# Low parts of two MLP products by an adding DMA, in a decoder block on one Trainium2 core

## The chip, the core and the metric

The kernel runs on one core of a Trainium2 chip. The core has a matrix engine (TensorE, PE in the profile), a vector engine (VectorE, DVE), a scalar engine (ScalarE, ACT), GpSimd (POOL) and SyncE (SP), which issues transfers. Each engine works through its own instructions in the order in which they stand, and waits on semaphores for the others. Sixteen DMA engines move data between HBM and the on-chip memory SBUF; products accumulate in PSUM banks.

The metric is the device time of one execution in microseconds (us). Before the change it is 862.61 us, the median of three runs (862.43 to 863.16).

## The reference

One decoder block over 512 tokens of width 1024, all in float32: two branches (stick-breaking attention, RWKV-7), a squared-ReLU MLP, a gated embedding and a final norm. The change lies in the MLP, whose second product is `... @ w_ff2`:

```python
D_MODEL = 1024; SEQ = 512; D_FF = 4 * D_MODEL
h = rms_norm(x, mlp_norm_g[i])
x = x + jnp.square(jax.nn.relu(h @ w_ff1[i])) @ w_ff2[i]     # the MLP
gate = jax.nn.sigmoid(rms_norm(x, ple_norm_g[i]) @ w_ple_gate[i])
x = x + gate * (p[i] @ w_ple_proj[i])
return rms_norm(x, final_norm_g)
```

## The kernel before

**Split operands.** TensorE multiplies in a short float format (`float32r`). To keep float32 accuracy each operand is two tiles, a high part (the value cast to `float32r`) and a low part (the value minus the high part, cast too), and each product is three matmuls: high by high, high by low, low by high.

**Weights.** They are cut into units of 128 x 1024 floats (512 KB). The list `seq` holds the order in which units are used. For a unit, `fetch_to` has SP load it from HBM into `w_raw` (four buffers), has ACT cast it into `w_hi` (line 221, three buffers), and has DVE subtract to make `w_lo` (line 222, three buffers). A cast therefore has to wait until PE is done with the unit three places earlier. `step` calls `fetch_to` after the third step of the unit in use, so that the next units are asked for ahead.

**The MLP.** The hidden width is worked through in four quarters (`qd` 0 to 3). In a quarter the first product makes 1024 hidden columns: pairs of units (`FF1`), some of them by a scheme with seven block products in place of eight (`seven`); the last pair of each quarter is always two whole units of 24 matmuls of 512 columns. Relu and square (`squared`, ACT) and sums and splits of the results (`operands`) follow.

The second product of a quarter (`FF2`) is seven block products (`seventh`, i = 0 to 6), each with two units (`p_` = 0 and 1): fourteen units in a row, each used by twelve matmuls of 512 columns (`rows3`, lines 252 to 254: high by high, low weights, low rows). Products 0 and 1 use units as they are loaded. Products 2 and 4 use sums of units that were prepared earlier in `B11a`, `B11b`, `B12a`, `B12b`. Products 3 and 6 subtract such a sum from the loaded unit first, and 5 uses its units as loaded. A unit is written (i, p_) here; those of products 0 and 1 are (0,0), (0,1), (1,0) and (1,1). In the trace their rows operands are named `fA` (products 0, 1 and 6) and `fS` (products 2 to 5).

**What sets the order.** The program is recorded in the order of the Python code, and a scheduler then places each engine's instructions by when it reckons them ready. So a change of one operation can move others on every engine. Nothing of the order is read for time here: times come from the trace.

The other work on ACT beside the casts, where products 0 and 1 begin: relu and square of the last `FF1` unit, the high parts of the rows (`fA`, `fS`), and in quarter 0 the high parts `tb` of sums of the normed input, which later quarters use.

Of the kernel before, what the change touches and what calls it, by code (L numbers as in the profile page):

```python
# [13 lines left out]
AF = mybir.ActivationFunctionType  # L14
ALU = mybir.AluOpType
# [25 lines left out]
U_PLE, U_QKV, U_RW, U_GSB, U_GRW, U_UPSB, U_UPRW, U_OUT, U_FF1, U_FF2, U_GATE = range(11)  # L41
# [50 lines left out]
def tile_block(ctx: ExitStack, tc: tile.TileContext, xT, xt, pT, wts, lora, cols_d, gfin_d, consts_d, out, dbg=None):  # L92
    nc = tc.nc
    act, dve, pool, pe, sync = nc.scalar, nc.vector, nc.gpsimd, nc.tensor, nc.sync
# [3 lines left out]
    def r32(ap):  # L98
        return ap.bitcast(F32)
# [34 lines left out]
    seq = []  # L134
# [31 lines left out]
    def unit(i):  # L166
        if seq[i][0] == U_FF2:
            return wts[UBASE[U_FF2] + seq[i][1] * 8 + FF2_FROM[seq[i][2]] + seq[i][3]]
        if seq[i][0] == U_S12:
            return wts[UBASE[U_FF1] + seq[i][1] * 8 + seq[i][2] + 4]  # L170
        return wts[UBASE[seq[i][0]] + seq[i][1]]

    def load_to(n):
        while len(loaded) < min(n, len(seq)):
            i = len(loaded)
            loaded.append(None)
            if seq[i] not in sources and seq[i][0] not in (U_S3, U_S4):
                loaded[i] = wpool.tile([P, 1024], F32, name="w_raw", bufs=4)
                sync.dma_start(out=loaded[i], in_=unit(i))
# [11 lines left out]
    def made(i):  # L191
        kind = seq[i][0]
        if seq[i] in sources:
            return sources[seq[i]]()
        if kind == U_S12:
            four_sums(i)
            return sums12[seq[i][1:]][:, 0:2].rearrange("p s x -> p (s x)")
        if kind == U_S3:
            return loaded[i - 1]
        if kind == U_S4:  # L200
            return sums12.pop(seq[i][1:])[:, 2]
        if seq[i] in changed:
            changed[seq[i]](loaded[i])
        return loaded[i]

    def fetch_to(n, ahead=0):
        while state["i"] < min(n, len(seq)):
            i = state["i"]
            state["i"] += 1
            load_to(i + 1 + ahead)  # L210
            raw = made(i)
            if seq[i] in homes:
                hi, lo = homes[seq[i]]()
            elif seq[i][0] == U_S4:
                hi = wpool.tile([P, 512], F32R, name="w_hi4", bufs=1)
                lo = wpool.tile([P, 512], F32R, name="w_lo4", bufs=1)
            else:
                hi = wpool.tile([P, 1024], F32R, name="w_hi")
                lo = wpool.tile([P, 1024], F32R, name="w_lo")
            with tc.issue_after(state["hx"]) if seq[i] == (U_FF1, 4) else nullcontext():  # L220
                state["cast"] = act.copy(out=hi, in_=raw).ins  # L221
            dve.tensor_tensor(out=lo, in0=raw, in1=r32(hi), op=ALU.subtract)  # L222
            ready.setdefault(seq[i], []).append((hi, lo))

    def weights(*u):
        assert seq[state["used"]] == u, (seq[state["used"]], u)
        state["used"] += 1
        fetch_to(state["used"])
        state["due"] = 3
        return ready[u].pop(0)  # L230
# [11 lines left out]
    def step():  # L242
        state["due"] -= 1
        if state["due"] == 0:
            fetch_to(state["used"] + AHEAD - 1, 1)
# [77 lines left out]
    with ExitStack() as sA:  # L323
# [43 lines left out]
        with ExitStack() as s1:  # L367
# [47 lines left out]
            for i in range(2):  # L415
                ready[seq[i]] = [tuple(first_w[i])]
            fetch_to(3)

            for k in range(KT):
# [1171 lines left out]
```

## Time and profile before

| What | Value |
|---|---|
| Time, median of three runs | 862.61 us (862.43 to 863.16) |
| Profiled execution: from its first to its last instruction (span) | 861.2 us |
| Granted TensorE clock, mean | 0.997 |
| PE busy / DVE busy / ACT busy / POOL busy | 845.6 / 716.8 / 497.2 / 74.4 us |
| DMA, mean rate | 131 GB/s |
| First `FF2` matmul of the four quarters, from the span's start | 522.7, 603.4, 682.8, 762.2 us |
| Transfers issued by POOL | none |

The profile has no time of the profiled execution other than its span; the median of the runs is 1.4 us longer than that span. "Busy" is the time in which an engine has an instruction under way. Matmuls overlap, so that one lasts 0.39 us but the next begins 0.23 us after it. In a timeline row the columns are the start and the length in us, the engine, the line, the operation, the tiles (out<-in), and in brackets the idle time before it with what ended it. Waits are what an engine idled for, in all, how often, and the longest. For a transfer, "to landing" is the time from its issue to the semaphore that says its data is there. Lines carry the numbers of the kernel before; in the kernel after the change those behind line 222 are four higher.

### The profile page before, as it was taken

What the parts mean: (1) busy time and instruction counts of PE and PEld (TensorE: products, weight loads), DVE (VectorE), ACT (ScalarE), POOL (GpSimd) and SP (SyncE); (2) the same over time, 40 slices, a digit from 0 to 9 for tenths busy, and PEclk for the clock granted to TensorE, in tenths of its full rate; (3) what the DMA queues carried; (4) which work ended last, traced back from release to release, by engine and by line L of the source; (5) the groups of instructions that cost most, each with busy time, mean ns of one, the idle gap of its engine ahead of it and who ended that gap; (6) DMA issues with size and microseconds to landing.
All of it is one profiled execution on the core that took longest, in us unless ns stands there. A gap on an engine that the chain in (4) does not pass through costs nothing.

```text
span 861.2 us, 14225 instructions
## 1 busy us (share of the span) xinstructions
PE 845.6 (98%) x5462; PEld 694.2 (81%) x5462; DVE 716.8 (83%) x1271; ACT 497.2 (58%) x777; POOL 74.4 (9%) x138
## 2 busy tenths in 40 slices
PE   8999999999999999999999999999999999999996
PEld 5778788877777777877888888889889889988885
DVE  7989987896987988867763599999889989998767
ACT  7878887744436253534555665457547744773843
POOL 1332431001202111020000000000000000000000
PEclk9999999999999999999999999999999999999998
DMA  8312212231221314428950643654364555444502
GB/s 319 100 49 62 87 62 85 74 99 51 62 88 37 111 63 138 159 86 277 324 186 20 245 123 100 217 172 143 118 205 133 161 188 166 140 144 128 192 23 98
DMA packets 37027, 112.67 MB, mean 131 GB/s; under 512 B 4192, under 2 KB 4192, under 8 KB 36960
## 3 DMA queue, kind: packets, MB, share of 16 engines
q1 hardware_dynamic: 36960, 111.76, 39.1%
q8 instruction: 43, 0.70, 0.3%
q14 instruction: 24, 0.20, 0.1%
HBM read 101.26 MB, written 10.49 MB: 130 GB/s over the span
## 4 chain that ended last, share of the span: by engine, by line
PE 83%; DVE 12%; issue 2%; ACT 1%; DMA 1%; SPq 0%; POOL 0%; POOLq 0%; DVEq 0%; ACTq 0%
PE ps_m L237 14%; PE ps_m L238 14%; PE ps_m L239 14%; PE ps_m L253 8%; PE ps_m L254 8%; PE ps_m L252 8%; DVE w_lo L222 2%; PE ps_g L863 1%; PE ps_o L543 1%; PE ps_s L991 1%; PE ps_z L551 1%; PE ps_c L982 1%; PE ps_g L953 1%; DVE LX L885 1%; DVE own L874 1%
## 5 line engine op out<-in xcount | busy, mean ns | idle before, releaser
L221 ACT CAST w_hi<-w_raw 128x1024 fp32r<-128x1024 f32 x131 | 137.4, 1051 | 160.1 <-PE ps_m L238 92.0
L222 DVE TENSOR_TENSOR w_lo<-w_raw,w_hi 128x1024 fp32r<-128x1024 f32 x131 | 159.8, 1223 | 26.6 <-ACT w_hi L221 26.0
L237 PE MATMUL ps_m<-h_hi,w_hi 128*128 128x512 f32 x320 | 130.5, 409 | 1.1 <-ACT h_hi L399 0.6
L239 PE MATMUL ps_m<-h_hi,w_lo 128*128 128x512 f32 x320 | 128.4, 401 | 0.0
L238 PE MATMUL ps_m<-h_lo,w_hi 128*128 128x512 f32 x320 | 128.0, 400 | 0.0
L238 PE MATMUL ps_m<-hx,w_hi 128*128 128x512 f32 (+1 forms) x224 | 77.1, 344 | 0.1
L237 PE MATMUL ps_m<-hx,w_hi 128*128 128x512 f32 (+1 forms) x224 | 77.1, 344 | 0.0
L239 PE MATMUL ps_m<-hx,w_lo 128*128 128x512 f32 (+1 forms) x224 | 77.0, 344 | 0.0
L237 PEld LDWEIGHTS ps_m<-h_hi,w_hi 128*128 128x128 f32 x320 | 60.7, 190 | 12.6 <-ACT h_hi L399 1.3
L239 PEld LDWEIGHTS ps_m<-h_hi,w_lo 128*128 128x128 f32 x320 | 60.2, 188 | 11.9
L238 PEld LDWEIGHTS ps_m<-h_lo,w_hi 128*128 128x128 f32 x320 | 60.4, 189 | 10.7 <-DVE h_lo L400 0.9
L253 PE MATMUL ps_m<-w_lo,fS 128*128 128x512 f32 x128 | 49.8, 389 | 0.0
L254 PE MATMUL ps_m<-w_hi,fS 128*128 128x512 f32 x128 | 49.8, 389 | 0.0
L252 PE MATMUL ps_m<-w_hi,fS 128*128 128x512 f32 x128 | 49.6, 389 | 0.0
L238 PEld LDWEIGHTS ps_m<-hx,w_hi 128*128 128x128 f32 x224 | 42.5, 190 | 5.3 <-DVE hx L1098 0.4
L237 PEld LDWEIGHTS ps_m<-hx,w_hi 128*128 128x128 f32 x224 | 42.5, 190 | 5.1 <-ACT hx L1097 0.2
L239 PEld LDWEIGHTS ps_m<-hx,w_lo 128*128 128x128 f32 x224 | 42.4, 190 | 5.0
L1456 POOL TENSOR_SCALAR r<-s 128x1 f32<-128x1 f32 x1 | 0.5, 517 | 475.3 <-DVE t L1436 475.3
L253 PE MATMUL ps_m<-w_lo,fA 128*128 128x512 f32 x96 | 37.7, 392 | 0.3 <-DVE w_lo L222 0.3
L254 PE MATMUL ps_m<-w_hi,fA 128*128 128x512 f32 x96 | 37.5, 391 | 0.0
L252 PE MATMUL ps_m<-w_hi,fA 128*128 128x512 f32 x96 | 37.4, 391 | 0.0
L1359 DVE TENSOR_TENSOR xs<-ps_m,xs 128x512 f32<-128x512 f32 x56 | 36.3, 682 | 0.2 <-PE ps_m L254 0.2
(405 smaller groups left out, 2083.9 us busy)
## 6 DMA issues: line engine op xcount, KB each, us to landing
w_raw<-in_wts_dram SPq DMA_DIRECT2D x146, 512.0 KB, 3.5
gates<-gg SPq DMA_DIRECT2D x16, 256.0 KB, 2.0
x_in<-in_xT_dram SPq DMA_DIRECT2D x8, 256.0 KB, 5.7
tmp<-gates SPq DMA_DIRECT2D x8, 256.0 KB, 3.2
upsb<-tmp SPq DMA_DIRECT2D x8, 256.0 KB, 4.6
ga<-upsb SPq DMA_DIRECT2D x8, 256.0 KB, 5.0
gb<-gates SPq DMA_DIRECT2D x8, 256.0 KB, 5.0
xs<-in_xt_dram SPq DMA_DIRECT2D x4, 512.0 KB, 5.3
```

What stands on the lines that cost most here:

```text
L221: state["cast"] = act.copy(out=hi, in_=raw).ins
L222: dve.tensor_tensor(out=lo, in0=raw, in1=r32(hi), op=ALU.subtract)
L237: pe.matmul(ps, wh, xh[:, k, t], start=first, stop=False, skip_group_check=skip)
L238: pe.matmul(ps, wh, xl[:, k, t], start=False, stop=False, skip_group_check=skip)
L239: pe.matmul(ps, wl, xh[:, k, t], start=False, stop=last, skip_group_check=skip)
L252: pe.matmul(ps, xh[:, k + j], wh, start=first and j == 0, stop=False, skip_group_check=True)
L253: pe.matmul(ps, xh[:, k + j], wl, start=False, stop=False, skip_group_check=True)
L254: pe.matmul(ps, xl[:, k + j], wh, start=False, stop=last and j == 1, skip_group_check=True)
L543: pe.matmul(ps_o[:, j * P:T], vv[:, j, hh, :, :].rearrange("p a d -> p (a d)"), part[:, ZB[j]:ZB[j] + ZN[j]], start=j == 2 and part is wh, ...
L551: pe.matmul(zt[b][:, :n], tri, part[:, s:s + n], start=False, stop=False, skip_group_check=True)
L863: last = pe.matmul(ps[rows, k], left[rows, k, :], rhs[rows, k], start=True, stop=True)
L1359: state["anchor"] = dve.tensor_tensor(out=xb, in0=pss[t2], in1=xb, op=ALU.add).ins
```

## The change

For the units of products 0 and 1 of the second MLP product, in all four quarters, `w_lo` is no longer made by DVE. ACT writes minus `w_hi` into `w_lo`, and then a DMA that POOL issues reads the raw unit from HBM a second time and adds it to what stands in `w_lo`. All other units are made as before. That is 4 units in each of 4 quarters: 16 DVE subtractions are gone, 16 ACT instructions and 16 transfers of 512 KB, issued by POOL, are added.

```diff
             with tc.issue_after(state["hx"]) if seq[i] == (U_FF1, 4) else nullcontext():
                 state["cast"] = act.copy(out=hi, in_=raw).ins
-            dve.tensor_tensor(out=lo, in0=raw, in1=r32(hi), op=ALU.subtract)
+            if seq[i][0] == U_FF2 and seq[i][2] in (0, 1):
+                act.activation(out=lo, in_=r32(hi), func=AF.Copy, scale=-1.0)
+                pool.dma_start(out=lo, in_=unit(i), accum_op=ALU.add)
+            else:
+                dve.tensor_tensor(out=lo, in0=raw, in1=r32(hi), op=ALU.subtract)
             ready.setdefault(seq[i], []).append((hi, lo))
```

The change also moves instructions. Three places show it.

On ACT, in quarter 0, where the second product begins. Before, from the cast of unit (1,0), `w_hi_5499`, on (`r_5439` is relu and square of the last `FF1` unit):

```order
L221 CAST w_hi_5499<-w_raw_5454 128x1024
L1250 ACTIVATE r_5439<-ps_m_5444 128x512
L1251 ACTIVATE r_5439<-r_5439 128x512
L1263 CAST tb0_5124<-tsum_5223 128x1024
L267 CAST fA20_5126<-r_5439 128x512
L221 CAST w_hi_5515<-w_raw_5497 128x1024
L221 CAST w_hi_5535<-B11a_5228 128x1024
L267 CAST fS0_5128<-sums_5477 128x1024
L221 CAST w_hi_5553<-B11b_5400 128x1024
```

And now, with the cast of (1,0) as the first row, `w_hi_5501`; (1,1) is `w_hi_5518`:

```order
L221 CAST w_hi_5501<-w_raw_5455 128x1024
L1267 CAST tb0_5124<-tsum_5223 128x1024
L1254 ACTIVATE r_5440<-ps_m_5445 128x512
L223 ACTIVATE w_lo_5502<-w_hi_5501 128x1024
L1255 ACTIVATE r_5440<-r_5440 128x512
L221 CAST w_hi_5518<-w_raw_5499 128x1024
L271 CAST fA20_5126<-r_5440 128x512
L223 ACTIVATE w_lo_5519<-w_hi_5518 128x1024
L271 CAST fS0_5128<-sums_5479 128x1024
L221 CAST w_hi_5539<-B11a_5228 128x1024
```

Line 223 is the new copy of minus high. The cast of `tb`, which stood behind relu and square, now stands ahead of them and of the copy for (1,0).

On ACT in quarter 2, from the cast of (1,0), `w_hi_6987`, on (quarters 1 and 3 read alike there, to the second copy):

```order
L221 CAST w_hi_6987<-w_raw_6941 128x1024
L1254 ACTIVATE r_6926<-ps_m_6931 128x512
L223 ACTIVATE w_lo_6988<-w_hi_6987 128x1024
L1255 ACTIVATE r_6926<-r_6926 128x512
L221 CAST w_hi_7004<-w_raw_6985 128x1024
L271 CAST fA20_5126<-r_6926 128x512
L271 CAST fS0_5128<-sums_6965 128x1024
L223 ACTIVATE w_lo_7005<-w_hi_7004 128x1024
```

No `tb` stands there; the copy for (1,0) comes behind relu, the one for (1,1) behind two casts of row operands.

On PE in quarter 0, unit (1,0), `w_hi_5499`, before:

```order
L252 MATMUL ps_m_5524<-w_hi_5499,fA20_5126 128x512
L253 MATMUL ps_m_5524<-w_lo_5500,fA20_5126 128x512
L254 MATMUL ps_m_5524<-w_hi_5499,fA21_5127 128x512
L252 MATMUL ps_m_5524<-w_hi_5499,fA20_5126 128x512
L253 MATMUL ps_m_5524<-w_lo_5500,fA20_5126 128x512
```

And as now placed:

```order
L256 MATMUL ps_m_5528<-w_hi_5501,fA20_5126 128x512
L256 MATMUL ps_m_5529<-w_hi_5501,fA20_5126 128x512
L257 MATMUL ps_m_5528<-w_lo_5502,fA20_5126 128x512
L258 MATMUL ps_m_5528<-w_hi_5501,fA21_5127 128x512
L256 MATMUL ps_m_5528<-w_hi_5501,fA20_5126 128x512
```

The row with `w_lo_5502` is the third of the unit; before, the low part was read by the second. Of unit (1,1) PE does the two first rows, then two rows (quarter 0) or six (the other quarters) of product 2, and only then the first row with its low part. On POOL, at the end of its queue, the transfers stand one behind another:

```order
L1002 TENSOR_SCALAR Sg<-S_1573,gc__3396 64x64 x2
L1002 TENSOR_SCALAR Sg<-S_1574,gc__3396 64x64 x2
L224 DMA w_lo<-in_wts_dram 128x1024 x16
L1460 TENSOR_SCALAR r_8157<-s_8156 128x1
L1461 TENSOR_SCALAR r_8157<-s_8156 128x1
```

Nothing else of POOL is queued between its last work of the RWKV branch and the end of the kernel.

## The prediction

> **What bounds the kernel now.** I read the busy times first, then the chain that ended last, then the stretches of the MLP, and last the waits of PE.
>
> ```profile
> PE 845.6 (98%) x5462; PEld 694.2 (81%) x5462; DVE 716.8 (83%) x1271; ACT 497.2 (58%) x777; POOL 74.4 (9%) x138
> ...
> PE 83%; DVE 12%; issue 2%; ACT 1%; DMA 1%; SPq 0%; POOL 0%; POOLq 0%; DVEq 0%; ACTq 0%
> ```
>
> PE is busy for 845.6 of 861.2 us. The chain gives DVE 12%, which might tempt one to relieve it. The stretches say where that matters (columns: stretch, its length, then busy time and count of PE, PE's loads, DVE, ACT, POOL, then the granted clock, DMA share and rate). The four are the second products of the four quarters:
>
> ```profile
> 522.70:559.00 36.30, 36.01 (x158) 29.36 (x157) 35.80 (x41) 18.12 (x20) 0.00 (x0) 1.00 0.47 153
> 603.40:640.00 36.60, 36.60 (x162) 30.16 (x162) 30.42 (x36) 17.32 (x18) 0.00 (x0) 1.00 0.51 169
> 682.80:719.00 36.20, 36.20 (x160) 29.84 (x159) 30.44 (x38) 16.83 (x18) 0.00 (x0) 1.00 0.54 170
> 762.20:799.00 36.80, 36.80 (x163) 30.35 (x162) 30.24 (x35) 18.30 (x19) 0.00 (x0) 1.00 0.40 122
> ...
> PE ps_m L253 <- DVE w_lo L222: 0.3, 1, 0.3
> ```
>
> DVE is nearly full in quarter 0 (35.80 of 36.30) and has about 6 us free in each of the others, yet PE has no hole except 0.3 us, once, for a low part of line 222. PE itself bounds the MLP, at full clock. So taking work from DVE can give back 0.3 us at most, and any low part that arrives late is paid in full, since PE runs in order and has no reserve.
>
> **The change part by part.** *Removed*: 16 DVE subtractions.
>
> ```profile
> L222 DVE TENSOR_TENSOR w_lo<-w_raw,w_hi 128x1024 fp32r<-128x1024 f32 x131 | 159.8, 1223 | 26.6 <-ACT w_hi L221 26.0
> ...
> L1319 ACT ACTIVATE r<-r 128x1024 f32<-128x1024 f32 x8 | 8.5, 1061 | 4.5 <-DVE r L1318 4.5
> ```
>
> 16 x 1.22 = 19.5 us of DVE, all beside PE: worth the 0.3 us above, no more. *Added on ACT*: 16 copies; the ACTIVATE of the same 128x1024 takes 1.06 us, so 17 us, of which ACT has the room (18 of 36 us busy). Without that room they would push casts back; what they do push is counted below. *Added on POOL and the DMA engines*: 16 transfers. POOL has nothing else queued there, and SP's queue is not passed.
>
> What decides is when the low part is there against when PE asks for it. A unit's cast has to wait for PE to release the buffer three units back. Unit (0,0) is cast two whole `FF1` units ahead of its use, 10.9 us, and (0,1) 8.2 us; (1,0) and (1,1) have only two `FF2` units ahead of them. ACT where quarters 0 and 2 start:
>
> ```profile
> 522.64 1.06 ACT L221 CAST w_hi<-w_raw 128x1024 fp32r<-128x1024 f32 x1 [1.84 <-PE ps_m L238]
> 523.60 0.59 ACT L1250 ACTIVATE r<-ps_m 128x512 f32<-128x512 f32 x1
> 524.22 0.63 ACT L1251 ACTIVATE r<-r 128x512 f32<-128x512 f32 x1
> 524.76 1.06 ACT L1263 CAST tb<-tsum 128x1024 fp32r<-128x1024 f32 x1
> ...
> 682.79 1.05 ACT L221 CAST w_hi<-w_raw 128x1024 fp32r<-128x1024 f32 x1 [1.61 <-PE ps_m L238]
> 683.75 0.59 ACT L1250 ACTIVATE r<-ps_m 128x512 f32<-128x512 f32 x1
> 684.37 0.63 ACT L1251 ACTIVATE r<-r 128x512 f32<-128x512 f32 x1
> ```
>
> and PE where unit (1,0) begins, in quarter 0 and in quarter 2, with the sum that `tb` waits for:
>
> ```profile
> 523.51 1.22 DVE L1221 TENSOR_TENSOR tsum<-tsum,hx 128x1024 f32<-128x1024 f32 x1
> ...
> 528.27 0.39 PE L252 MATMUL ps_m<-w_hi,fA 128*128 128x512 f32 x1
> 528.49 0.39 PE L253 MATMUL ps_m<-w_lo,fA 128*128 128x512 f32 x1
> ...
> 688.42 0.39 PE L252 MATMUL ps_m<-w_hi,fA 128*128 128x512 f32 x1
> 688.65 0.39 PE L253 MATMUL ps_m<-w_lo,fA 128*128 128x512 f32 x1
> ```
>
> Call L the time from the end of the copy of minus high to the moment when PE sees the sum landed.
>
> Quarters 1 to 3 (read in quarter 2; the first `FF2` matmul is at 682.83): in the new order cast, relu, copy. The copy takes the place of the square, 684.37, and ends at 685.43. PE now puts two high matmuls first, so that the first low one is due at 688.42 + 2 x 0.23 = 688.88. The stall is L - 3.45.
>
> Quarter 0: in the new order the `tb` cast stands ahead of relu and of the copy. It waits for `tsum`, which ended at 524.73; one subtraction (1.2 us) ahead of it on DVE goes away and a short sum waits for the later square, so I take 523.7 for it, and the `tb` cast ends at 524.75, relu at 525.4, the copy at 526.5. The low part is due at 528.27 + 0.46 = 528.73. The stall is L - 2.2.
>
> Unit (1,1): its cast waits for the square behind the copy. In quarter 2 that gives square 686.0, cast 687.0, two row casts 688.55, copy 689.6. PE, once (1,0) has landed at 685.43 + L, does ten more matmuls of it, two of (1,1) and six of product 2, 18 x 0.23 = 4.1 us, and asks at 689.5 + L; the sum lands at 689.6 + L. In quarter 0: copy until 529.85 against 526.5 + 14 x 0.23 = 529.7. About 0.1 us each. That is, the second sum travels while the first is awaited and computed, and costs next to nothing more. What stands behind the copies on ACT, the casts for product 2, ends by 690 to 692 and is asked for at about 688.2 + L: covered, as long as L is over 4, by the stall itself.
>
> Together: 4 L - 2.2 - 3 x 3.45 + 0.4 - 0.3 = 4 L - 12.5 us, where no L makes a quarter negative.
>
> L is what this trace does not have: there is no transfer issued by POOL in it, and none that adds. The nearest rows are SP's plain loads of the same 512 KB (issue; minimum, median, maximum to landing), the same size issued in pairs, the rate at which the DMA engines run when full, and POOL's shortest instruction:
>
> ```profile
> L179 SPq DMA_DIRECT2D w_raw<-in_wts_dram x76: 327/328/504, 486.4 to 817.0; - x76
> ...
> DMA to landing us min/median/max: 3.3/3.5/7.1
> ...
> DMA to landing us min/median/max: 3.7/4.9/5.2
> ...
> 12.00:16.00 4.00, 3.98 (x18) 2.98 (x17) 4.00 (x8) 4.00 (x8) 0.00 (x0) 1.00 1.04 417
> ...
> 854.65 0.52 POOL L1456 TENSOR_SCALAR r<-s 128x1 f32<-128x1 f32 x1 [475.27 <-DVE t L1436]
> ```
>
> From below L is 3.3, the quickest plain load: an adding transfer reads the same bytes from HBM and more. From above I take two loads in turn, one for each operand, the second at the slowest landing seen: 3.5 + 7.1 = 10.6, as if nothing overlapped. Between them: 3.5 for a plain load, 1.26 for a second operand of 524 KB at 417 GB/s (it has to be read out of `w_lo`), 0.5 for POOL where SP needs 0.33 (POOL's shortest row), and 0.7, half of the 1.4 us by which paired loads land later, since loads for the next units fall in the same stretch (DMA share 0.40 to 0.54). That is 6.0 us, an estimate.
>
> The page "DMA: Bandwidth & Descriptors" of the Trainium skill (section "Anatomy of one DMA — SWDGE (gpsimd) path") speaks against the change too, but more mildly: for a transfer issued by GpSimd it gives 2.0 us plus the bytes at 436 GB/s, which for twice 512 KB would be an estimate of L = 4.4 and 4 x 4.4 - 12.5 = 5 us lost. No run here shows such a transfer yet.
>
> With L = 6.0 the stalls are 3.8 us in quarter 0 and 2.6 us in each other quarter, and the sum 4 x 6.0 - 12.5 = 11.5 us. The profiled span of 861.2 becomes 872.7, and the median of the runs, which stands 1.4 us above that span, 862.6 + 11.5 = **874.1 us**.
>
> **The rivals.**
>
> *A. The add lands like a plain load* (L 3.3 to 4.9). For it: DMA engines stand half idle in these stretches (shares 0.40 to 0.54). Against it: it has an operand more to read, and POOL to pass. Time: quarter 0 loses 1.1 to 2.7, the others nothing to 1.45 each, so 863.7 to 869.7.
>
> *B. The add is much slower than two reads, or the stall costs the clock* (L 7.5 to 10.6, or a stall that throttles). For it: the clock falls soon after PE stops.
>
> ```profile
> 1.31 5.29 PE L382 MATMUL ps_z<-warm 128*128 128x512 bf16 x12 [1.31 <-POOL warm L379]
> ...
> 853.40:856.60 3.20, 0.12 (x2) 0.00 (x0) 2.84 (x11) 2.57 (x5) 0.99 (x2) 0.96 0.22 82
> 856.60:861.20 4.60, 0.00 (x0) 0.00 (x0) 0.94 (x2) 0.72 (x1) 0.00 (x0) 0.50 0.46 171
> ```
>
> PE's last matmul ended at 853.5 and the granted clock was 0.50 some 3 us later. Coming back costs about what the start shows: 12 matmuls in 5.29 us, 0.44 each against 0.23 later, 2.6 us lost. At L = 6.0 only quarter 0 stands idle for longer than 3 us; from L = 6.5 on all do, and then 4 x 2.6 = 10.4 us come on top: 886.5 at L = 6.5. Without the clock, L = 7.5 to 10.6 gives 880 to 892. Against it: the slowest load of 512 KB in the MLP took 7.1.
>
> The page "TensorE: Matmul & The Clock Gate" (section "Part 1: The HAM clock gate (the "warmup" mystery)") of the Trainium skill has the rule for this rival: after an idle window of about 3.4 us the clock is halved, and as long a busy one restores it. The end of this trace agrees, with the fall after some 3 us; by the page's window one fall would cost 1.7 us in place of 2.6, and four would give 883.
>
> *C. Not slower: the sums land in time.* One mechanism: the copy of minus high is done by 685.4 in quarters 1 to 3 and PE asks at 688.9, so that a transfer with L under 2.2 in quarter 0 and under 3.45 in the others costs nothing, and PE keeps at most its 0.3 us: 862.3. With L up to 3.4 the loss stays at 1.2 us, within what can be told. For it: 3.3 was seen. Against it: that was the quickest of 84 plain loads. Faster than 0.3 us it cannot get, because PE had no more holes; only a different order elsewhere could do that.
>
> **How the numbers follow.** The forecast (L 4.9 to 7.5 without the clock, 869.7 to 880) has a chance of 0.5, A 0.2, B 0.17, C 0.13. Differences under 0.2%, 1.7 us, can't be told from none. Faster by more has 0.03 (C's remainder), within has 0.10 of C and 0.02 of A, 0.12, and slower the rest, 0.85. The range reaches from 864.5 (A at L = 3.6) to 889 (B at L = 9.7): it leaves out most of C and the far end of B. The predicted time is that of the forecast.
>
> **What would show it.** Right: PE idle in front of the matmul with `w_lo` and `fA` of the second pair of units, eight waits or fewer, the longest in quarter 0, about 3.8 us and three of 2.6, put down to a transfer; transfers of POOL that land 5 to 7 us after the copy; DVE about 20 us less busy and ACT 17 more; everything outside `FF2` as before. Wrong: PE as gapless as before (C); waits in front of (0,0) or (0,1), which have 8 us and more, if the transfers wait for one another or POOL is slow at issuing them; a granted clock under 1 inside the MLP (B); or waits of PE on ACT or DVE at product 2, which would mean that the copies push casts back further than I reckoned.

## The result, and the profile after

The kernel after the change takes 884.02 us (median of four runs, 882.24 to 888.73), beside 862.88 us for the kernel before on the same chip. The ratio is 1.0254, with a 95% interval of 1.0230 to 1.0278: slower, by 21.1 us. Forecast were 874.1 us, 11.5 us more than before, and a range of 864.5 to 889. One execution of the kernel with product 0 alone (below) took 1676 us, with every matmul twice as long, for a reason that nothing here shows; the times below leave it out, and the 8.5 us in one expectation, which take it in, are 7.6 without it.

The profiled execution is the longest of the four, 888.73 us with a span of 887.0 us, 25.8 us over the span before. Its busy times, the chain that ended last, and the row of the adding transfers among the queues (packets, MB, their time as a share of 16 engines' span):

```profile
PE 854.2 (96%) x5462; PEld 698.2 (79%) x5462; DVE 701.7 (79%) x1255; ACT 510.6 (58%) x793; POOL 88.6 (10%) x154
...
q0 software_dynamic: 2304, 8.39, 5.6%
...
PE 75%; issue 9%; DVE 8%; DMA 5%; ACT 1%; SPq 0%; POOLq 0%; POOL 0%; DVEq 0%; ACTq 0%
```

DVE is 15 us less busy, ACT 13 more (forecast were 20 and 17), and neither shows in the time. PE is busy for 8.6 us longer with the same 5462 matmuls, and 17.0 us of idle time are new, in front of one line (PE's waits: us in all, how often, the longest):

```profile
PE ps_m L257 <- DMA w_lo<-in_wts_dram: 17.0, 8, 4.8
```

17.0 and 8.6 are the 25.8 us, nearly. The eight waits in PE's timeline (line 257 takes the low weights; in brackets the idle time before):

```profile
533.60 0.50 PE L257 MATMUL ps_m<-w_lo,fA 128*128 128x512 f32 x1 [3.04 <-DMA w_lo<-in_wts_dram]
614.29 0.50 PE L257 MATMUL ps_m<-w_lo,fA 128*128 128x512 f32 x1 [1.60 <-DMA w_lo<-in_wts_dram]
618.34 0.50 PE L257 MATMUL ps_m<-w_lo,fA 128*128 128x512 f32 x1 [0.78 <-DMA w_lo<-in_wts_dram]
692.99 0.50 PE L257 MATMUL ps_m<-w_lo,fA 128*128 128x512 f32 x1 [0.52 <-DMA w_lo<-in_wts_dram]
696.95 0.50 PE L257 MATMUL ps_m<-w_lo,fA 128*128 128x512 f32 x1 [0.92 <-DMA w_lo<-in_wts_dram]
705.07 0.80 PE L257 MATMUL ps_m<-w_lo,fA 128*128 128x512 f32 x1 [4.84 <-DMA w_lo<-in_wts_dram]
787.37 0.55 PE L257 MATMUL ps_m<-w_lo,fA 128*128 128x512 f32 x1 [3.71 <-DMA w_lo<-in_wts_dram]
793.79 0.50 PE L257 MATMUL ps_m<-w_lo,fA 128*128 128x512 f32 x1 [1.58 <-DMA w_lo<-in_wts_dram]
```

Four of them, at 533.60, 618.34, 705.07 and 793.79, are at unit (1,0), as forecast, 10.2 us together. The other four are at (0,0) and (0,1), which I had called covered. The copies and the transfers themselves (an instruction's nanoseconds: minimum, median, maximum; then us from issue to landing):

```profile
L223 ACT ACTIVATE w_lo<-w_hi 128x1024 fp32r<-128x1024 f32 x16 | 16.8, 1053 | 0.1
...
L224 POOL DMA_DIRECT2D w_lo<-in_wts_dram x16: 865/865/1031, 516.3 to 787.3; - x16
...
DMA to landing us min/median/max: 5.5/7.3/10.3
```

The copies cost what was reckoned, 1.05 us each. POOL starts a transfer 0.3 us after the copy's end, so the median L is 7.6 us where I took 6.0. Transfer by transfer, L was 5.8, 6.3, 9.6 and 10.8 us at (1,0) in quarters 0 to 3, a mean of 8.1, and 5.8 to 9.4 at the others.

PE's longer busy time is mostly a slower clock. The stretches of PE after three of the waits (length, PE busy and matmuls, granted clock, DMA share, rate):

```profile
535.10:538.50 3.40, 3.40 (x9) 0.50 0.62 122
538.50:541.90 3.40, 3.40 (x16) 1.00 0.00 0
702.30:709.10 6.80, 4.03 (x10) 0.50 0.45 84
787.70:791.10 3.40, 3.40 (x9) 0.50 1.02 257
```

In 3.4 us PE does 9 matmuls at half clock and 16 at the full one. One more such stretch, at 306 us, lies ahead of the MLP, where the change adds nothing; the second product of quarter 0 began 1.7 us later than before (524.36 against 522.70). In these stretches PE did 3.4 + 3.4 + 4.0 + 3.4 us of work, and half of it, 7.1 us, is what the clock cost. The rest of the 8.6 us goes with the waits: the matmul ahead of a wait runs out alone, 0.39 less 0.23 us each time.

### The profile page after: what moved, and what is told of

Read it like the earlier page. It is cut to its first block, busy times and chain, and to the rows that moved or that the text cites. A ratio compares the mean times of both kernels' runs of the same rounds, so it can differ in the third digit from the quotient of the medians.

```text
span 887.0 us, 14281 instructions
## 1 busy us (share of the span) xinstructions
PE 854.2 (96%) x5462; PEld 698.2 (79%) x5462; DVE 701.7 (79%) x1255; ACT 510.6 (58%) x793; POOL 88.6 (10%) x154
## 3 DMA queue, kind: packets, MB, share of 16 engines
q0 software_dynamic: 2304, 8.39, 5.6%
## 4 chain that ended last, share of the span: by engine, by line
PE 75%; issue 9%; DVE 8%; DMA 5%; ACT 1%; SPq 0%; POOLq 0%; POOL 0%; DVEq 0%; ACTq 0%
PE ps_m L241 12%; PE ps_m L242 12%; PE ps_m L243 12%; PE ps_m L257 8%; PE ps_m L258 8%; PE ps_m L256 7%; DMA w_lo<-in_wts_dram 4%; PE ps_g L867 1%; PE ps_o L547 1%; PE ps_s L995 1%; PE ps_c L986 1%; DVE w_lo L226 1%; PE ps_z L555 1%; PE ps_g L957 1%; DVE LX L889 1%
## 5 line engine op out<-in xcount | busy, mean ns | idle before, releaser
L226 DVE TENSOR_TENSOR w_lo<-w_raw,w_hi 128x1024 fp32r<-128x1024 f32 x115 | 140.5, 1224 | 19.8 <-ACT w_hi L221 18.8
L257 PE MATMUL ps_m<-w_lo,fA 128*128 128x512 f32 x96 | 40.4, 421 | 17.0 <-DMA w_lo<-in_wts_dram 17.0
L224 POOL DMA_DIRECT2D w_lo<-in_wts_dram x16 | 14.0, 878 | 393.1 <-ACT w_lo L223 167.7
L258 PE MATMUL ps_m<-w_hi,fA 128*128 128x512 f32 x96 | 39.5, 412 | 0.0
L257 PEld LDWEIGHTS ps_m<-w_lo,fA 128*128 128x128 f32 x96 | 19.3, 201 | 24.9 <-DMA w_lo<-in_wts_dram 20.8
```

The costliest lines, as they stand in the source:

```text
L224: pool.dma_start(out=lo, in_=unit(i), accum_op=ALU.add)
L257: pe.matmul(ps, xh[:, k + j], wl, start=False, stop=False, skip_group_check=True)
L258: pe.matmul(ps, xl[:, k + j], wh, start=False, stop=last and j == 1, skip_group_check=True)
```

## The experiments

Three questions stood open: is the add slow or the way over POOL (the copy and the half-size runs); is it only the landing against the lead, or do traffic, copies and POOL cost something by themselves (one product alone, the first product's units, the later low matmuls, fewer loads beside); and what the clock adds (the fillers). Each expectation says what its two theories are.

### The same transfers without the addition

```diff
-                pool.dma_start(out=lo, in_=unit(i), accum_op=ALU.add)
+                pool.dma_start(out=lo, in_=unit(i))
```

> All sixteen transfers stay with POOL, at the same size and place, but they write the raw unit over the copy of minus high in place of adding to it. Left out is the addition, so the low part holds the raw weights here; nothing else differs. Theory 1 (the add is slow: its second operand has to be read and written back by the DMA engines): landings come down to those of SP's plain loads plus POOL's 0.5 us more of issue, 4.0 to 5.5 us after the copy; stalls of 1 to 3 us a quarter, 4 L - 12.5 = 3.5 to 9.5 us, no fall of the clock: 866 to 872 us. Theory 2 (what is slow is the way over POOL, whether it adds or not): landings of 5.5 to 10.3 us as before, and 880 to 886 us.

Measured: 869.63 us (868.19 to 870.62), before 863.29, ratio 1.0069 (1.0041 to 1.0096). Its page and the answer on the transfers:

```profile
q0 software_dynamic: 2304, 8.39, 3.2%
...
L224 POOL DMA_DIRECT2D w_lo<-in_wts_dram x16: 527/527/757, 513.6 to 772.1; - x16
...
DMA to landing us min/median/max: 3.7/4.5/7.1
...
PE ps_m L257 <- DMA w_lo<-in_wts_dram: 5.1, 4, 1.7
...
770.21 0.50 PE L257 MATMUL ps_m<-w_lo,fA 128*128 128x512 f32 x1 [1.67 <-DMA w_lo<-in_wts_dram]
```

Theory 1 as it stood there, that the add is slow, holds. With as many bytes in as many packets, the packets take 3.2% in place of 5.6% of the engines' time: 16 x 866.4 x 0.032 / 2304 = 0.19 us each against 16 x 887.0 x 0.056 / 2304 = 0.34. POOL's instruction falls from 865 to 527 ns, the median landing from 7.3 to 4.5 us. Three of the four waits that stay are at (1,0), in quarters 0 to 2; the longest, shown above, is at (0,1) in quarter 3, where L was 7.4, and (1,0) of that quarter waited for nothing. The clock is whole. L at (1,0) was 4.0, 4.5, 5.1 and 5.4 us, a mean of 4.7, and the prediction's 4 L - 12.5 gives 6.5 us for it; the runs lost 6.3 by their median, and the profiled one 5.2.

The Trainium skill, page "DMA: Bandwidth & Descriptors", section "Anatomy of one DMA — SWDGE (gpsimd) path", has 2.0 us plus bytes at 436 GB/s for a transfer of POOL, 3.2 us for this one, an estimate; the fastest of these plain ones took 3.7 and the median 4.5, and the adding ones 5.5 and 7.3.

### Half the columns by the add, half by DVE

```diff
-                act.activation(out=lo, in_=r32(hi), func=AF.Copy, scale=-1.0)
-                pool.dma_start(out=lo, in_=unit(i), accum_op=ALU.add)
+                act.activation(out=lo[:, 0:512], in_=r32(hi[:, 0:512]), func=AF.Copy, scale=-1.0)
+                pool.dma_start(out=lo[:, 0:512], in_=unit(i)[:, 0:512], accum_op=ALU.add)
+                dve.tensor_tensor(out=lo[:, 512:1024], in0=raw[:, 512:1024], in1=r32(hi[:, 512:1024]), op=ALU.subtract)
```

> For the same sixteen units only the first 512 columns of the low part come by the copy and the adding transfer (256 KB, rows of 2 KB), the other 512 by DVE's subtraction. Theory 1 (the time in the air grows with the bytes, as a packet that adds takes 0.35 us for 4 KB where one that only writes takes 0.19): half the packet time, 8 x 0.17 = 1.4 us less, and a copy half as long, 0.5 us less: landings of 4 to 6 us, waits of about 1 us a quarter: 865 to 871 us. Theory 2 (the way over POOL costs the same for any size: its instruction, the first packet 1.6 us later, the number of packets): landings stay above 5 us and only the 0.5 us of the copy is won per wait, 877 to 882 us.

Measured: 875.7 us (874.72 to 880.88), before 863.23, ratio 1.0158 (1.0126 to 1.0190): between the two theories.

```profile
q0 software_dynamic: 2304, 4.20, 3.1%
...
DMA to landing us min/median/max: 3.9/5.2/6.4
...
PE ps_m L258 <- DMA w_lo<-in_wts_dram: 9.6, 8, 2.2
```

Half the bytes land 2.1 us sooner by the median, and a packet takes 0.19 us, as long as a plain one of twice the size. But over 5 us stay for a quarter of a megabyte. The landings, 3.9 to 6.4 us, are close to theory 1's 4 to 6, but the waits are not: 9.6 us in place of some 4, and neither theory's time was right. On a straight line through the two sizes, an estimate, the part that grows with the bytes is 2.1 of the 5.2 us here and 4.2 of the 7.3 at full size; some 3 us stay, which no run here splits up (POOL, the first packet, the wait for other transfers).

### One product at a time

Product 1 alone (`== 0` in place of `== 1` for product 0 alone):

```diff
-            if seq[i][0] == U_FF2 and seq[i][2] in (0, 1):
+            if seq[i][0] == U_FF2 and seq[i][2] == 1:
```

> Only units (1,0) and (1,1) get their low parts by the adding transfer; those of product 0 are DVE's again. Theory 1 (own landing time against own lead): (1,0) is asked for 2.2 us after the copy in quarter 0 and 3.45 us in the others, its sums keep landing 5.8 to 10.8 us after the copy, and the stalls sum to about 11 us as in the trace after the change, or more in quarters 1 and 3, where waits at product 0 had given (1,0) more time: 4 x 8.1 - 12.5 = 20 us, 875 to 885 us. Theory 2 (pile-up): (1,0) is now the first adding transfer of its quarter and lands after 5.5 to 6.5 us in all four: 4 x 6 - 12.5 = 11.5 us, 872 to 877 us, and only quarter 0 stands long enough for the clock to fall.

Measured: 879.48 us (877.05 to 881.11), ratio 1.0177 (1.0147 to 1.0206), 16 us more than before. The landings and the waits in PE's timeline:

```profile
DMA to landing us min/median/max: 5.5/6.3/8.5
```

```profile
530.31 0.50 PE L257 MATMUL ps_m<-w_lo,fA 128*128 128x512 f32 x1 [2.46 <-DMA w_lo<-in_wts_dram]
614.45 0.51 PE L257 MATMUL ps_m<-w_lo,fA 128*128 128x512 f32 x1 [2.04 <-DMA w_lo<-in_wts_dram]
619.93 0.50 PE L257 MATMUL ps_m<-w_lo,fA 128*128 128x512 f32 x1 [1.06 <-DMA w_lo<-in_wts_dram]
697.76 0.50 PE L257 MATMUL ps_m<-w_lo,fA 128*128 128x512 f32 x1 [2.19 <-DMA w_lo<-in_wts_dram]
784.08 0.79 PE L257 MATMUL ps_m<-w_lo,fA 128*128 128x512 f32 x1 [5.05 <-DMA w_lo<-in_wts_dram]
...
690.77 1.05 ACT L223 ACTIVATE w_lo<-w_hi 128x1024 fp32r<-128x1024 f32 x1
```

In quarter 2 the copy ends at 691.82 and PE goes on at 697.76, 5.9 us later. L at (1,0) was 6.2, 5.8, 5.9 and 8.8 us; with the waits counted from matmul start to matmul start, less the usual 0.23 (2.6, 2.2, 2.35, 5.2), the lead (from the copy's end to PE's asking) comes out at 3.5 us in all four quarters. That is the prediction's 3.45 of quarters 1 to 3, and 1.3 more than its 2.2 for quarter 0. (In quarter 0 the cast of `tb` stands behind the copy in this kernel, not ahead of it.) As to the pile-up: three of four L were about 6, as theory 2 had it, but two of these had been so with product 0's transfers, too (5.8 and 6.3). Quarter 2's fell from 9.6, and quarter 3's only from 10.8 to 8.8. The time lies in the middle of theory 1's range and above theory 2's, among other things because even the waits of 2.46 and 2.19 us were followed by half clock (below).

Product 0 alone:

> Only the four first units of the second product in each quarter, (0,0) and (0,1), get their low parts by the adding transfer; those of product 1 go back to DVE. In the trace after the change the waits at these units were 1.8 us in quarter 1, 1.7 in quarter 2 and 3.9 in quarter 3, because the sums took 7.4 to 9.4 us from the copy of minus high where I had counted on 8 us and more of lead being enough. Theory 1 (each unit pays by its own landing time against its own lead, and the transfers do not hinder each other): these waits stay, 5 to 8 us, with perhaps one fall of the granted clock (1.7 us): 867 to 873 us. Theory 2 (they were late because the eight adding transfers of a quarter pile up): with half as many the landings come down to the 5.5 to 6.5 us of the quietest ones, and as (0,0) and (0,1) are the first in the pile already, most of it is only seen in the other half; here 863 to 866 us.

Measured: 870.93 us (870.83 to 872.63), ratio 1.0086 (1.0058 to 1.0114), 7.6 us more than before. (A quarter has four adding transfers, not eight as this expectation says.) The same kernel, profiled again:

> Product 0's units alone once more, for its profile: the one taken before was of an execution in which every matmul took twice as long, where nothing waited. From the timed runs of that kernel (8.5 us above before): theory 1 (own landing against own lead) has waits of 5 to 7 us in front of (0,0) and (0,1) in quarters 1 to 3 and none in quarter 0, and one fall of the clock, and nothing else different from before: 869 to 873 us.

Measured: 870.59 us. Its waits:

```profile
686.82 0.50 PE L257 MATMUL ps_m<-w_lo,fA 128*128 128x512 f32 x1 [1.56 <-DMA w_lo<-in_wts_dram]
769.84 0.79 PE L257 MATMUL ps_m<-w_lo,fA 128*128 128x512 f32 x1 [3.38 <-DMA w_lo<-in_wts_dram]
```

Theory 1: (0,1) was late by 1.6 and 3.4 us, at L of 7.7 and 9.5, and two windows of 3.4 us at half clock came with the second wait. 4.9 us of waits are a little less than the 5 to 7 expected; quarter 1 waited for nothing this time, at L = 5.8. These L are no lower than with product 1's transfers present, so theory 2's pile-up isn't seen here. The two halves cost 7.6 and 16.2 us, 23.8 together, and 21.1 in one kernel, a difference within the intervals of the three runs. What the traces do show is that a wait at (0,1) lets (1,0)'s sum travel meanwhile: with both products, (1,0)'s lead in quarters 1 to 3 was 5.4, 4.6 and 9.1 us, against 3.5 with product 1 alone.

### The same recipe where the lead is long

```diff
-            if seq[i][0] == U_FF2 and seq[i][2] in (0, 1):
+            if seq[i][0] == U_FF1 and seq[i][1] in (1, 2, 3, 5, 6, 7):
```

> The same recipe (copy of minus high on ACT, adding transfer by POOL) for six other units, the whole FF1 units 1, 2, 3, 5, 6 and 7 of quarter 0; FF2 goes back to DVE altogether. Two units of 5.5 us each stand between cast and use, so that the lead is about 9.8 us behind the copy. Theory 1 (a late landing is the only thing that costs): landings of 5.5 to 7 us are covered, 862.9 us, within 1.5 us of before. Theory 2 (each such transfer costs something wherever it stands, by its traffic, by the ACT copy or by POOL): six of sixteen of the 21 us, 8 us, 870 us.

Measured: 867.56 us (866.06 to 868.49), ratio 1.0043 (1.0031 to 1.0055). One wait, then 3.4 us at half clock:

```profile
DMA to landing us min/median/max: 7.0/8.3/10.1
...
493.75 0.50 PE L243 MATMUL ps_m<-hx,w_lo 128*128 128x512 f32 x1 [3.80 <-DMA w_lo<-in_wts_dram]
```

My lead was wrong for the first of the six: its copy ended at 484.18, PE asked for it 5.8 us later, and it landed after 9.5, with 1.8 MB of SP's loads for the start of the MLP beside it. The other five took 7.3 to 10.4 us and PE did not wait for them. So the same kernel without that unit:

> As the run with the six units of FF1, without its first one (FF1 unit 1 of quarter 0), the only one at which PE waited there: 3.8 us, with SP's loads of the MLP's start beside the transfer (1.8 MB until it had landed, 9.5 us after the copy). The other five took 7.3 to 10.4 us and PE did not wait for them. Theory 1 (only a late landing costs): no waits, 862.5 to 864 us. Theory 2 (traffic, ACT copies or POOL cost something by themselves): five sixths of the 4.3 us of that run, 866 to 867 us.

Measured: 864.5 us (863.48 to 866.03), ratio 1.0017 (1.0008 to 1.0027), 1.3 us more than before, just above what theory 1 gave, which had no wait at all.

```profile
PE ps_m L243 <- DMA w_lo<-in_wts_dram: 1.2, 1, 1.2
```

Again the first transfer was late (L of 10.3 us at a lead of 9, 2.4 MB beside it). Its 1.2 us are nearly the whole 1.3, so that the other four, the traffic, their copies on ACT and POOL's work cost nothing that can be told. Theory 2, 866 to 867 us, is out for these units.

### The low matmuls later

```diff
             pe.matmul(ps, xh[:, k + j], wh, start=first and j == 0, stop=False, skip_group_check=True)
-            pe.matmul(ps, xh[:, k + j], wl, start=False, stop=False, skip_group_check=True)
+            if low:
+                pe.matmul(ps, xh[:, k + j], wl, start=False, stop=False, skip_group_check=True)
...
-                rows3(pss[t2], w, op, t2, p_ * 2, first and p_ == 0, p_ == 1)
+                rows3(pss[t2], w, op, t2, p_ * 2, first and p_ == 0, p_ == 1, low=i > 1)
+            if i < 2:
+                for t2 in range(2):
+                    for j in range(2):
+                        pe.matmul(pss[t2], op[0][:, p_ * 2 + j, t2 * P:(t2 + 1) * P], w[1][:, j * 512:(j + 1) * 512],
+                                  start=False, stop=p_ == 1 and j == 1, skip_group_check=True)
```

> The change as it is, but PE takes the four matmuls with the low weights of each unit of products 0 and 1 after the other eight, so that the low part is asked for six matmuls, 1.38 us, later; transfers, bytes and matmuls are the same. Theory 1 (each wait is landing time less lead): every wait of the trace after the change is 1.38 us shorter. In the starts of the matmuls these were 3.2 us in quarter 0, 1.76 and 0.94 in quarter 1, 0.68, 1.07 and 5.0 in quarter 2, 3.88 and 1.74 in quarter 3; they become 1.8, 0.4, 0, 0, 0, 3.6, 2.5, 0.4, 8.7 us in all, with one or two falls of the clock (1.7 us each): 872 to 877 us. Theory 2 (what PE gains at one unit it loses at the next, as casts and transfers follow PE's releases): the sum of waits stays near 17 us, 881 to 885 us.

Measured: 882.47 us (879.91 to 883.48), before 863.23, ratio 1.0216 (1.0193 to 1.0239). Theory 1's number failed. Theory 2's range has it, but not its reason in full: the waits fell from 17.0 to 13.7 us.

```profile
PE ps_m L1362 <- DMA w_lo<-in_wts_dram: 13.7, 7, 3.8
...
617.14 1.38 PE L1362 MATMUL ps_m<-w_lo,fA 128*128 128x512 f32 x3 [3.17 <-DMA w_lo<-in_wts_dram]
702.60 0.63 PE L1362 MATMUL ps_m<-w_lo,fA 128*128 128x512 f32 x1 [3.83 <-DMA w_lo<-in_wts_dram]
```

What failed is the subtraction from every wait. A quarter is delayed by its latest sum, whose transfer starts at its copy's end, whatever PE waits for at (0,1): in quarters 1 and 3 (1,0)'s copy ended 2.5 us after the first `FF2` matmul in both kernels, though the waits at (0,1) had fallen from 1.8 and 3.9 us to 0.5 and 1.9. So a wait at (0,1) that is saved can come back at (1,0). Taken once per quarter, 4 x 1.38 = 5.5 us were to be had at most. The four sums of the waits per quarter (start to start, less 0.23), 3.2, 2.7, 6.8 and 5.6 us after the change, were 3.0, 3.8, 4.0 and 4.1 here, 3.4 less; quarter 1 got worse, with an L at (1,0) of 8.8 us in that execution where it had been 6.3. Three windows at half clock followed the longer waits here, too.

### Fillers against the clock

```diff
+                fill = i == 1 and p_ == 0 and t2 == 0 and qd in (0, 2)
+                for n in range(12 if fill else 0):
+                    pe.matmul(pss[0], op[0][:, 0, 0:P], w[0][:, 0:512], start=n == 0, stop=False, skip_group_check=True)
-                rows3(pss[t2], w, op, t2, p_ * 2, first and p_ == 0, p_ == 1)
+                rows3(pss[t2], w, op, t2, p_ * 2, first and p_ == 0 and not fill, p_ == 1)
```

> The change as it is, and in quarters 0 and 2 PE gets 12 more matmuls of 512 columns at the start of unit (1,0), 2.76 us of work each time, that stand in the time in which PE waited there (3.2 and 5.0 us); transfers and casts are untouched. These matmuls add the high products of one block to product 1 twelve times more, so the result of product 1 is not the reference's. Theory 1 (PE's idle time makes the granted clock fall, and each fall costs its 1.7 us beside the wait): the fillers lie inside waits and cost nothing, the waits there shrink to 0.4 and 2.2 us, the falls behind them (one in quarter 0, two in quarter 2) go, and the kernel gets faster by 3 to 5 us through doing more: 879 to 881 us, mean clock 0.995 or more. Theory 2 (the falls are not worth anything, or come from something other than idle time): 884 to 886 us, with the same falls.

Measured: 883.82 us (881.01 to 886.2), before 862.4, ratio 1.0253 (1.0235 to 1.0271). Half of theory 1 held: the mean clock was 0.995 to 0.996 in all its runs, against 0.988 to 0.992 without fillers, and behind both fillers it stayed whole; the profile's one fall in the MLP is in quarter 1, which has no filler. The other half, the gain, did not come, and the time lies in neither theory's range, just under theory 2's, whose falls did not stay either. Quarter 0 shows one reason (the waits at (1,0) and (1,1), and the granted clock behind the first):

```profile
531.26 0.50 PE L257 MATMUL ps_m<-w_lo,fA 128*128 128x512 f32 x1 [0.47 <-DMA w_lo<-in_wts_dram]
535.68 0.50 PE L257 MATMUL ps_m<-w_lo,fA 128*128 128x512 f32 x1 [1.41 <-DMA w_lo<-in_wts_dram]
...
533.20:536.60 3.40, 1.99 (x9) 1.00 0.54 106
```

At full clock PE now comes too early for (1,1), and waits 1.41 us; in the kernel after the change it worked through (1,0) at half clock there (from 535.1) and found the sum of (1,1) landed. So part of what the clock took had been cover for the next sum. The rest is not settled: in this execution (1,0) landed after 6.4 us in quarter 2, not 9.6, so the filler's 2.76 us were no longer all inside a wait.

### Fewer loads beside

```diff
-            for i, n in ((2, "T2"), (4, "T3")):
+            for i, n in ((2, "T2"), (4, "T3"), (3, "T2"), (5, "T3"), (6, "T2")):
```

> The change as it is, but the units of products 3, 5 and 6 are not loaded: they are cast from the sums that stand in the chip already. Left out are six of a quarter's transfers by SP and four of DVE's subtractions; what PE multiplies there is wrong. The sixteen adding transfers stay. Theory 1 (the spread of the landings, 5.5 to 10.3 us, comes from SP's loads on the same DMA engines): with these loads gone around (1,0) and (1,1), (1,0) lands after 5.5 to 6.5 us in quarters 2 and 3, too, where it took 9.6 and 10.8 us after the copy: 4 x 6 - 12.5 = 11.5 us, 872 to 877 us. Theory 2 (what slows them is only the other adding transfers just ahead of them, or POOL): L at (1,0) of quarters 2 and 3 stays at 8.5 us and more, 880 to 885 us.

Measured: 887.04 us (884.41 to 887.9), before 862.4, ratio 1.0276 (1.0258 to 1.0295).

```profile
DMA to landing us min/median/max: 5.2/6.8/9.0
...
PE ps_m L257 <- DMA w_lo<-in_wts_dram: 16.1, 8, 4.2
```

This did not test what it should. SP's later loads moved up into the room: beside the sum of (1,0) in quarters 1 to 3 there were still 1.0 MB of its packets until the landing, against 0.9, 0.9 and 1.4 in the change, and L was 7.6, 7.9 and 9.5 us. It does not tell the theories apart.

## Why the prediction was right, and where its size was off

**Direction and place.** PE is the bound, what DVE gained is worth nothing, and a late low part is paid by PE: eight waits, all put down to the transfer, and DVE's 15 us invisible. Without the add, 6.3 of the 21.1 us stay. The recipe on five units of `FF1` in place of sixteen of `FF2`, where most sums were in time, cost 1.3 us.

**What came was rival B.** The time is in the range, but not in the forecast's own band, 869.7 to 880: with a mean L of 8.1 at (1,0) it is in that of B (L of 7.5 to 10.6, 880 to 892), which had a chance of 0.17. And two of the four signs named as wrong are there, waits at (0,0) and (0,1), and a granted clock under 1 inside the MLP.

**The formula.** 4 L - 12.5 with the mean L at (1,0): plain copies, L = 4.7, 6.5 us against 6.3 measured; product 1 alone, L = 6.6, 14 against 16.2; the change, L = 8.1, 20 against 21.1. The first and the last agreement are partly luck. Of the four waits of the plain copies one was at (0,1). And in the profile of the change, 25.8 us longer than before, the waits at (1,0) were only 10.2 us, as waits at product 0, 6.8 us, had lengthened its lead; the clock's 7.1 us are most of the rest, and the formula has neither.

**The term that was mis-sized** is the second operand of the add. Of L = 6.0, the parts 3.5 + 0.5 + 0.7 = 4.7 were meant for a transfer of POOL without an add; the copies measured just this, 4.7 at (1,0). The add itself I priced at 1.26 us, 524 KB at the rate of full DMA engines. It cost 2.8 us by the median landing (7.3 against 4.5) and 3.4 at (1,0) (8.1 against 4.7). The reading was wrong, not only the rate: the operand does not follow once behind the data. Each packet takes 0.15 us longer, 1.4 us over the nine that each of 16 engines has of a transfer (2304 / 256), POOL's instruction takes 0.34 us longer, and what lasts longer overlaps with the next transfer and with SP's loads; that this last part makes up the remaining 1.1 us is argued, not shown.

**Covered units that were not.** "(0,0) and (0,1) have 8 us and more" counted from the cast. The time that matters starts at the end of the copy, some 2.4 us later, and was 5.6 to 6.6 us at the waits of (0,1), where L was 7.6 to 9.4. At (0,0) it was 8.6 in quarter 2, and L 9.3.

**Quarter 0** was to stall most, 3.8 us, because of `tb`. It stalled 3.0; the lead was 2.6 us there, not 2.2, and 3.5 with product 1 alone, where `tb` does not stand ahead of the copy. The longest waits came in quarters 2 and 3, with the latest landings.

**(1,1) at 0.1 us** held in the kernel after the change, in quarter 0 with the help of half clock, and not in some of its relatives: 1.06 us in quarter 1 with product 1 alone, 1.41 in quarter 0 with the fillers.

**Rival B's second half came true below its price.** It was to begin where PE stands idle for over 3 us. With product 1 alone a wait of 2.19 us was enough. In the profile of the change it cost 5.4 us of PE's time in the MLP, 7.1 with the stretch at 306 us, against the 10.4 of the prediction; the fillers show that part of it would have been waited anyway.

**ACT and DVE at product 2**: no wait there, as forecast.

## What to carry to other kernels

Count a lead from the last step that must be done before the transfer can start, and price an adding transfer by a run of one: here 7.3 us for 512 KB, where a plain one of the same queue took 4.5. Where the consumer has no reserve, relieving a busy engine beside it gives nothing, and waits within a group are not independent: one that is saved at an early unit can come back at the next. With a lead of 7.7 us and more behind the copy, nine of ten such transfers for `FF1` cost next to nothing, and the tenth, at 9 us, was 1.2 us late; the longest L seen was 10.8 us.

## What the runs showed of the hardware

**The clock falls in fixed windows.** With product 1 alone, half clock began at 531.1, 698.4 and 783.7 us, 49 and 25 times 3.413 us apart, and lasted 3.413 us each time. Around the first (PE busy and matmuls, granted clock):

```profile
527.70:531.10 3.40, 0.94 (x4) 1.00 0.95 241
531.10:534.50 3.40, 3.40 (x10) 0.51 0.79 149
534.50:537.90 3.40, 3.40 (x16) 0.99 0.06 11
```

A window that was mostly idle is followed by one at half clock. Over the traces with a fall in the MLP, windows of the MLP at full clock with 1.9 us or more of idle time on this grid were followed by a fall, and those with 1.6 us or less were not. Ahead of the MLP there was one fall, in the kernel after the change, behind a window with only 1.2 us of idle time, which this does not explain. The Trainium skill, page "TensorE: Matmul & The Clock Gate", section "Part 1: The HAM clock gate (the "warmup" mystery)", has this window, 3413 ns and running freely, and the traces agree; they add that it need not be idle throughout, so that a wait of 2.2 us did it here.

**The last of the 16 parts is what varies.** The first engine's part of an adding transfer landed 4.8 to 5.6 us after its issue in 72 of 91 cases, the last 5.2 to 10.3. Of these 91 transfers in eight traces, the nine with at most 0.39 MB of SP's packets in their first 5 us landed within 6.5 us, and those with more, from 5.3 to 10.3. So loads beside go along with late landings, but do not decide them, and the one run that was to take them away failed to. What sets a landing in its range is open.
